# A hybrid attention trunk: 64-row score products of branches A and B become 128-row products

## The chip, the cores and the metric

The kernel runs on one core of a Trainium2 chip. The metric is the device time of one execution in microseconds (us); lower is better. The engines are TensorE (PE in the views, its weight loads PEld), VectorE (DVE), ScalarE (ACT), GpSimd (POOL) and SyncE (SP, whose queue issues the weight transfers).

## The reference

Two layers of an encoder block over 256 tokens of width 2048, in float32. One normalised input feeds three attention branches; each is gated, projected and summed, and an output projection ends the layer. The change touches the scores of branches A and B. Branch A (first lines) has 8 heads of 128 position-free and 64 rotary channels, with one rotary key `kr` for all heads; branch B has 8 heads with two softmax maps (`c`) of 64 channels each:

```python
sc = (jnp.einsum('bqhd,bkhd->bhqk', qn_b, kn)
      + jnp.einsum('bqhr,bkr->bhqk', qr_b, kr)).astype(jnp.float32) * scale
...
sc = jnp.einsum('bqhcd,bkhcd->bhcqk', q_b, k).astype(jnp.float32) * scale
mask = _chunk_causal_mask(i * Q_BLOCK, Q_BLOCK, s_len)
p = jax.nn.softmax(jnp.where(mask, sc, -jnp.inf), axis=-1)
a = p[:, :, 0] - lam * p[:, :, 1]
return jnp.einsum('bhqk,bkhe->bqhe', a.astype(v.dtype), v)
```

Branch C is an attention over 128 channels per head with a position bias. It has no 64-channel part.

## The kernel before, in words

Every product is made from split operands: a value is written as a high part and a low part, each exact in the matmul's input format, and a product of two such values is high times high, high times low and low times high.

The big work is `matunit`: 256 tokens times a weight of K rows and up to 512 columns. Weights come in blocks of 256 rows (512 KB) on SP's queue into four buffers (`wr`). ScalarE rounds a block to its high part (`wh`, L146), VectorE subtracts to get the low part (`wl`, L147), three buffers each, and TensorE makes twelve products of 512 columns from a block (L155 to L157). Each layer runs some fifty such units.

The attention of a branch is done in two halves of four heads. For a half, `qk_natural` and `rope` normalise and rotate queries and keys with tokens in the partitions, `to_transposed` turns them on TensorE (L197), and a split function takes them out of PSUM as high and low parts. Then for each head `scores` (L276) multiplies a stationary query slice of 128 tokens by the keys: 128 key columns for the first 128 tokens, 256 for the second. `softmax_exp` takes the row minimum on VectorE (L287) and the exponential on ScalarE (L289). In branch B, `diff_half` combines the two maps of a head on VectorE (L367); the combined map is transposed (L297) and multiplied by the values (L314).

A head of branch B has only 64 channels per map, so its high and low parts share one 128-row tile. `split_stacked` puts the query's high part in one half of the rows and its low part in the other. `split_twice` puts the key's high part in both halves, so one 128-row product of the two gives (high + low of the query) times the high of the key. The remaining query high times key low is a product of its own, over 64 rows:

```python
q, k = op["q"][m][:, hl, :], op["k"][m][:, hl, :]
return [(q, k), (q[hi], kl[hi, hl, :])]
```

`hi` is the half of the rows that holds the query's high part: rows 0 to 63 for map 0, rows 64 to 127 for map 1. The rotary part of branch A is built in the same way: `krt[:, 0, :]` is the high part of the shared rotary key and `krt[:, 1, :]` its low part. That key is transposed from a tile that already holds it twice, so both parts fill all 128 rows.

In the names, `l0b0` is layer 0, branch B, half 0; `l0b_s` are scores, `l0b0k` the key's high parts, `l0b0kl` its low parts, `l0b0q` the stacked queries, `l0b0z_p` the sums of the gate unit that runs beside the scores, `l0b0z_h` and `l0b0z_l` its split weights.

A scheduler that simulates the timeline fixes the order on each engine when the kernel is built; each engine then runs its own list in order and waits on semaphores. It places scores and transposes between the products of the next `matunit`. Tiles of the attention come from a ring of eleven buffers (`att`), so the twelfth tile waits until the first is read for the last time. Transposes share two PSUM buffers (`ps_t`), scores another two (`ps_s`).

Of the kernel before, what the change touches and what calls it, by code (L numbers as in the profile page):

```python
# [8 lines left out]
F32 = mybir.dt.float32  # L9
F32R = mybir.dt.float32r  # L10
AF = mybir.ActivationFunctionType
# [31 lines left out]
def stream_plan():  # L43
    """The order in which weight blocks are consumed: (source, column selector, K, N)."""
    order = []
    for l in range(DEPTH):
        def win(name, lo, n):
            order.append(("w_in", l, lo, DM, n))
        win("cq", 0, 512)
        win("ckv", 512, 320)  # L50
        win("az", 832, 512)
        order.append(("uq", l, 0, 512, 512))
        order.append(("uq", l, 1024, 512, 512))
        order.append(("ukv", l, 0, 256, 512))
        order.append(("ukv", l, 1024, 256, 512))
        win("az", 832 + 512, 512)
        order.append(("uq", l, 512, 512, 512))
        order.append(("ukv", l, 512, 256, 512))
        order.append(("ukv", l, 1536, 256, 512))
        qb = 1856  # L60
        for hf in range(2):
            for s in (1, 0, 2, 3):
                win("b", qb + s * BW + hf * 512, 512)
        gb = 1856 + 8 * BW
        for j in range(4):
            win("g", gb + j * 512, 512)
            order.append(("br0", l, j * 512, BW, 512))
        qc = 1856 + 4 * BW
        for hf in range(2):
            for s in (1, 0, 2, 3):  # L70
                win("c", qc + s * BW + hf * 512, 512)
        for n in (1, 2):
            for j in range(4):
                win("g", gb + n * DM + j * 512, 512)
                order.append((f"br{n}", l, j * 512, BW, 512))
        for j in range(4):
            order.append(("out", l, j * 512, DM, 512))
    return order
# [3 lines left out]
def trunk_kernel(ctx: ExitStack, tc: tile.TileContext, x, xT, w, cols, rows, tab, bias, ident_d, out):  # L82
    nc = tc.nc
# [19 lines left out]

    # ---------------------------------------------------------------- loads that come first
    colt = const.tile([P, DEPTH, NCOL], F32, name="colt")
# [14 lines left out]

    # keeps the array's clock up while the first loads are on their way
    warm = xgp.tile([P, 512], F32R, tag="xl3", name="warm")
# [4 lines left out]

    # ---------------------------------------------------------------- weight stream
    state = {"off": 0}

    def matunit(lhs, K, N, name, pre=None):
        """x-stationary product [256 tokens, N] over K, three exact passes of split operands."""
        ps = [ps_m.tile([P, 512], F32, tag="mm", name=f"{name}_p{t}") for t in range(NT)]
# [26 lines left out]
    def split(dh, dl, src, gain=None):  # L160
        """dh + dl = src * gain, both representable in float32r."""
        if gain is None:
# [7 lines left out]
    def split_stacked(d0, d1, src, gain=None):  # L170
        """Two 64-row operands of src: d0 = [high; low] of rows 0-63, d1 = [low; high] of rows 64-127."""
        a, b = slice(0, 64), slice(64, P)
# [8 lines left out]

    def split_twice(d0, d1, dl, src, gain):
        """d0 = [high; high] of rows 0-63, d1 the same of rows 64-127, dl the low parts in place."""
        a, b = slice(0, 64), slice(64, P)
        for hi, lo, d in ((a, b, d0), (b, a, d1)):
            nc.scalar.activation(d[hi], src[hi], AF.Copy, scale=gain[hi])
            nc.scalar.activation(d[lo], src[hi], AF.Copy, scale=gain[hi])
            nc.vector.scalar_tensor_tensor(out=dl[hi], in0=src[hi], scalar=gain[hi], in1=d[hi].bitcast(F32),
                                           op0=ALU.mult, op1=ALU.subtract)

    def to_transposed(src, nblk, dh, dl, gain, name, per_block=False, put=None):
        """src(t) [128 tokens, nblk*128] -> dh, dl [128, nblk, 256]; put(blocks, psum) replaces the plain split."""
        for b0 in range(0, nblk, 2):
# [13 lines left out]
    def rstd(ss, n, width, name):  # L207
        """(ss / width + eps) ** -0.5 over [128, n], in place."""
        nc.gpsimd.tensor_scalar(out=ss, in0=ss, scalar1=1.0 / width, scalar2=EPS, op0=ALU.mult, op1=ALU.add)
        nc.gpsimd.tensor_tensor(out=ss, in0=ss, in1=mhalf[:, :n], op=ALU.pow)  # L210

    def qk_natural(ps, gs, rcol, name):
        """per-head RMS normalisation of a [256, 512] product -> two natural tiles."""
        ng = 512 // gs
# [22 lines left out]
    def rope(dst, src, ctab, stab, ng, half, eng, name):  # L237
        """dst = src * ctab + swap(src) * stab over [128, ng, 2*half]."""
        shp = [P, ng, 2 * half]
# [24 lines left out]

    # ---------------------------------------------------------------- attention
    def scores(parts, name):
        """-scores of one head: [128 q, 0:128] for tokens 0-127, [128 q, 128:384] for tokens 128-255.

        parts: (stationary, moving) pairs whose products add up."""
        s = ps_s.tile([P, 384], F32, tag="s", name=name)  # L270
# [11 lines left out]
    def softmax_exp(s, add, mx, sums, name):  # L282
        """exp(score - max) with row sums; add(t) is subtracted from the scores."""
        p = wk.tile([P, 384], F32, tag="p", name=name, bufs=3)
# [8 lines left out]
    def p_transposed(p, name):  # L293
        """p [128 q, 384] -> split [128 k, 384]: columns are (k0, q0), (k0, q1), (k1, q1)."""
        pt = ps_t.tile([P, 512], F32, tag="t", name=f"{name}_pt")
# [7 lines left out]
    def attend(p, vh, vl, hl, name):  # L303
        """p [128 q, 384] times V of head hl of the half -> PSUM [128 q, tile, 128]."""
        ph, pl = p_transposed(p, name)
# [11 lines left out]
    def attend_transposed(p, vh, vl, hl, name):  # L317
        """the same product as PSUM [128 dv, 256 q]."""
        ph, pl = p_transposed(p, name)
# [11 lines left out]
    def simple_half(z, parts, vh, vl, add, name):  # L331
        """softmax attention of four heads -> transposed attention * z [128, 4, 256]."""
        zt = zp.tile([P, HH, SEQ], F32, tag="z", name=f"{name}zt")
# [47 lines left out]

    # ---------------------------------------------------------------- layers
    xg_next = None
# [3 lines left out]
    for l in range(DEPTH):  # L387
# [7 lines left out]

        # the normalised input and its first product
        if l == 0:
# [11 lines left out]
        def first_norm(rcol):  # L409
            """r of the first layer from the transposed x: squares summed over blocks, then over partitions."""  # L410
            acc = wk.tile([P, 384], F32, tag="p", name="xacc", bufs=3)[:, :SEQ]
# [21 lines left out]

        # the layer's gains, rotary tables and lambda
        rowt = wk.tile([P, 2, 512], F32, tag="g", name=f"rowt{l}").rearrange("p a b -> p (a b)")
# [26 lines left out]

        # ------------------------------------------------------------ branch A
        ss = sm.tile([P, NT], F32, tag="sscq", name=f"sscq{l}")
# [61 lines left out]
        for hf in range(2):  # L526
# [21 lines left out]
            def parts(hl):  # L548
                hi = slice((hl % 2) * 64, (hl % 2) * 64 + 64)
                qs = qr[hf][:, (hl % 2) * 2 + hl // 2, :]  # L550
                return three(qh[:, hl, :], ql[:, hl, :], kh[:, hl, :], kl[:, hl, :]) + [
                    (qs, krt[:, 0, :]), (qs[hi], krt[hi, 1, :])]

# [3 lines left out]

        # ------------------------------------------------------------ branch B
        zb = [None, None]
        for hf in range(2):  # L560
            n = f"l{l}b{hf}"
            op = {}
            for i, nm in ((1, "k"), (0, "q")):
# [6 lines left out]
                if nm == "k":  # L570
                    kl = att_tile(f"{n}kl")
                    put = lambda bs, pt: split_twice(d[0][:, bs, :], d[1][:, bs, :], kl[:, bs, :], pt, cg[:, 4:5])
                else:
# [6 lines left out]
            def bparts(hl, m):  # L580
                hi = slice(m * 64, m * 64 + 64)
                q, k = op["q"][m][:, hl, :], op["k"][m][:, hl, :]
                return [(q, k), (q[hi], kl[hi, hl, :])]

            diff_half(zb[hf], bparts, vh, vl, nlam, n)

        # ------------------------------------------------------------ gates, branch products
        yacc = bigp.tile([P, NT, DM], F32, tag="big", name=f"yacc{l}")
# [25 lines left out]

        # ------------------------------------------------------------ branch C
        zc = [None, None]
# [30 lines left out]

        # ------------------------------------------------------------ output projection, residual
        xres = bigp.tile([P, NT, DM], F32, tag="big", name=f"xres{l}")
# [102 lines left out]
```

## Time and profile before

| | |
|---|---|
| median of 3 runs | 2074.09 us (2073.89 to 2075.56) |
| the profiled execution, first to last instruction | 2074.0 us |
| TensorE busy | 2061.1 us, 9612 products |
| TensorE's weight loads busy | 1705.3 us |
| VectorE busy | 1200.8 us |
| ScalarE busy | 1117.7 us |
| GpSimd busy | 230.2 us |

The time that is on record for the profiled execution is its span; it lies 0.1 us from the median, so sums are made against it directly. A product's busy time on TensorE runs past the start of the next one, since products are pipelined; the pace of the engine is read from the distance between starts. A weight load (PEld) belongs to each product and normally runs while the product before it streams.

### The profile page before, as it was taken

How to read it: one execution, taken by the hardware profiler on the slowest of the kernel's cores; microseconds unless marked ns; L12 is line 12 of the kernel's file. 1: busy time of each engine (PE TensorE's matmuls, PEld its weight loads, DVE VectorE, ACT ScalarE, POOL GpSimd, SP SyncE). 2: the span in 40 equal slices, each digit the busy share in tenths (PEclk: the TensorE clock that was granted, in tenths of full speed). 3: DMA queues.
4: the chain of work that ended last, by engine and by line, in shares of the span. 5: the costliest groups of instructions: out<-in, count | busy, mean ns of one | idle time of the engine just before them, and what ended most of it. 6: DMA issues, size and time to landing. Idle time of an engine off the chain costs nothing.

```text
span 2074.0 us, 25839 instructions
## 1 busy us (share of the span) xinstructions
PE 2061.1 (99%) x9612; PEld 1705.3 (82%) x9612; DVE 1200.8 (58%) x1558; ACT 1117.7 (54%) x1606; POOL 230.2 (11%) x373
## 2 busy tenths in 40 slices
PE   8999999999999999999999999999999999999999
PEld 7888787888888888888888887878888888888887
DVE  6666666545655545555557666664455555455554
ACT  6666766444565544445456667564445555444443
POOL 4323032000200000000013130400001000000000
PEclk9999999999999999999999999999999999999999
DMA  6544445455555565556665444545556555655574
GB/s 221 189 153 143 152 156 186 161 193 189 192 170 181 165 197 192 190 191 239 207 190 181 147 148 145 170 163 173 193 187 194 168 181 172 194 193 185 191 243 153
DMA packets 106909, 375.27 MB, mean 181 GB/s; under 512 B 11920, under 2 KB 16016, under 8 KB 106272
## 3 DMA queue, kind: packets, MB, share of 16 engines
q1 hardware_dynamic: 104864, 365.18, 53.7%
q0 software_dynamic: 1920, 8.46, 1.3%
q8 instruction: 75, 1.23, 0.3%
q14 instruction: 50, 0.41, 0.1%
HBM read 369.39 MB, written 4.19 MB: 180 GB/s over the span
## 4 chain that ended last, share of the span: by engine, by line
PE 96%; POOL 1%; ACT 1%; DVE 1%; issue 0%; DMA 0%; SPq 0%; POOLq 0%; ACTq 0%; DVEq 0%
PE l0g_p L155 4%; PE l1g_p L155 4%; PE l1g_p L156 4%; PE l0g_p L156 4%; PE l0g_p L157 4%; PE l1g_p L157 4%; PE l0o_p L155 1%; PE l0o_p L156 1%; PE l0o_p L157 1%; PE l1o_p L155 1%; PE l1o_p L156 1%; PE l1o_p L157 1%; PE l0b_s L276 1%; PE l1b_s L276 1%; PE l0az_p L157 1%; PE l1az_p L156 1%
## 5 line engine op out<-in xcount | busy, mean ns | idle before, releaser
L147 DVE TENSOR_TENSOR l1g_l<-l1g_r,l1g_h 128x1024 fp32r<-128x1024 f32 x96 | 117.4, 1224 | 107.9 <-ACT l1g_h L146 107.8
L147 DVE TENSOR_TENSOR l0g_l<-l0g_r,l0g_h 128x1024 fp32r<-128x1024 f32 x96 | 117.4, 1224 | 107.9 <-ACT l0g_h L146 107.8
L146 ACT CAST l0g_h<-l0g_r 128x1024 fp32r<-128x1024 f32 x96 | 101.1, 1053 | 139.3 <-PE l0g_p L157 86.4
L146 ACT CAST l1g_h<-l1g_r 128x1024 fp32r<-128x1024 f32 x96 | 101.1, 1053 | 139.3 <-PE l1g_p L157 86.4
L156 PE MATMUL l1g_p<-l1g_l,xh 128*128 128x512 f32 x384 | 150.2, 391 | 0.0
L156 PE MATMUL l0g_p<-l0g_l,xh 128*128 128x512 f32 x384 | 150.2, 391 | 0.0
L157 PE MATMUL l1g_p<-l1g_h,xl 128*128 128x512 f32 x384 | 150.0, 391 | 0.0
L157 PE MATMUL l0g_p<-l0g_h,xl 128*128 128x512 f32 x384 | 150.0, 391 | 0.0
L155 PE MATMUL l1g_p<-l1g_h,xh 128*128 128x512 f32 x384 | 136.6, 391 | 0.0
L155 PE MATMUL l0g_p<-l0g_h,xh 128*128 128x512 f32 x384 | 136.6, 391 | 0.0
L155 PEld LDWEIGHTS l1g_p<-l1g_h,xh 128*128 128x128 f32 x384 | 72.0, 188 | 15.0
L155 PEld LDWEIGHTS l0g_p<-l0g_h,xh 128*128 128x128 f32 x384 | 72.1, 188 | 14.9
L157 PEld LDWEIGHTS l0g_p<-l0g_h,xl 128*128 128x128 f32 x384 | 72.1, 188 | 14.7
L157 PEld LDWEIGHTS l1g_p<-l1g_h,xl 128*128 128x128 f32 x384 | 72.1, 188 | 14.8
L156 PEld LDWEIGHTS l0g_p<-l0g_l,xh 128*128 128x128 f32 x384 | 72.1, 188 | 14.6
L156 PEld LDWEIGHTS l1g_p<-l1g_l,xh 128*128 128x128 f32 x384 | 72.1, 188 | 14.6
L147 DVE TENSOR_TENSOR l1o_l<-l1o_r,l1o_h 128x1024 fp32r<-128x1024 f32 x32 | 39.2, 1224 | 41.7 <-ACT l1o_h L146 41.7
L146 ACT CAST l1o_h<-l1o_r 128x1024 fp32r<-128x1024 f32 x32 | 33.8, 1055 | 53.1 <-PE l1o_p L157 45.9
L147 DVE TENSOR_TENSOR l0o_l<-l0o_r,l0o_h 128x1024 fp32r<-128x1024 f32 x32 | 39.2, 1224 | 36.1 <-ACT l0o_h L146 36.1
L146 ACT CAST l0o_h<-l0o_r 128x1024 fp32r<-128x1024 f32 x32 | 33.7, 1054 | 40.8 <-PE l0o_p L157 30.8
L650 POOL DMA_DIRECT2D xres<-x x1 | 0.8, 768 | 316.5 <-PE l0n2j3yT_t L197 316.5
L650 POOL DMA_DIRECT2D xres<-xscr x1 | 0.8, 768 | 316.5 <-PE l1n2j3yT_t L197 316.5
(1632 smaller groups left out, 5985.7 us busy)
## 6 DMA issues: line engine op xcount, KB each, us to landing
l0g_r<-w SPq DMA_DIRECT2D x96, 512.0 KB, 3.4
l1g_r<-w SPq DMA_DIRECT2D x96, 512.0 KB, 3.4
l0o_r<-w SPq DMA_DIRECT2D x32, 512.0 KB, 3.5
l1o_r<-w SPq DMA_DIRECT2D x32, 512.0 KB, 3.8
l0az_r<-w SPq DMA_DIRECT2D x16, 512.0 KB, 3.8
l1az_r<-w SPq DMA_DIRECT2D x16, 512.0 KB, 3.9
l0b0k_r<-w SPq DMA_DIRECT2D x8, 512.0 KB, 3.4
l0b0q_r<-w SPq DMA_DIRECT2D x8, 512.0 KB, 3.4
```

The costliest lines, as they stand in the source:

```text
L146: nc.scalar.copy(wh[:, ks, :N], wr[:, ks, :N])
L147: nc.vector.tensor_tensor(out=wl[:, ks, :N], in0=wr[:, ks, :N], in1=wh[:, ks, :N].bitcast(F32), op=ALU.subtract)
L155: nc.tensor.matmul(ps[t][:, :N], h[:, ts], wh[:, k2, :N], start=first, stop=False)
L156: nc.tensor.matmul(ps[t][:, :N], h[:, ts], wl[:, k2, :N], start=False, stop=False)
L157: nc.tensor.matmul(ps[t][:, :N], lo[:, ts], wh[:, k2, :N], start=False, stop=last)
L276: nc.tensor.matmul(o, a[:, qs], b[:, :kn], start=i == 0, stop=i == len(parts) - 1)
L650: nc.gpsimd.dma_start(xres, x_src.rearrange("(t p) d -> p t d", p=P))
```

## The change

The key's low part, like its high part, is now written to both halves of a 128-row tile, and the last product of each score group takes all 128 rows of the stacked query. The sum gains the product of the two low parts. In branch A the low part is in both halves already, so only the slices go. In branch B `split_twice` writes two tiles of low parts, one for each map, in place of one; its copies and subtractions alternate between ScalarE and VectorE. Comments and docstrings were dropped as well, which the diff leaves out.

```diff
-    def split_twice(d0, d1, dl, src, gain):
+    def split_twice(d0, d1, l0, l1, src, gain):
         a, b = slice(0, 64), slice(64, P)
-        for hi, lo, d in ((a, b, d0), (b, a, d1)):
-            nc.scalar.activation(d[hi], src[hi], AF.Copy, scale=gain[hi])
-            nc.scalar.activation(d[lo], src[hi], AF.Copy, scale=gain[hi])
-            nc.vector.scalar_tensor_tensor(out=dl[hi], in0=src[hi], scalar=gain[hi], in1=d[hi].bitcast(F32),
-                                           op0=ALU.mult, op1=ALU.subtract)
+        for hi, lo, d, dl in ((a, b, d0, l0), (b, a, d1, l1)):
+            for o in (hi, lo):
+                nc.scalar.activation(d[o], src[hi], AF.Copy, scale=gain[hi])
+                nc.vector.scalar_tensor_tensor(out=dl[o], in0=src[hi], scalar=gain[hi],
+                                               in1=d[hi].bitcast(F32), op0=ALU.mult, op1=ALU.subtract)
...
             def parts(hl):
-                hi = slice((hl % 2) * 64, (hl % 2) * 64 + 64)
                 qs = qr[hf][:, (hl % 2) * 2 + hl // 2, :]
                 return three(qh[:, hl, :], ql[:, hl, :], kh[:, hl, :], kl[:, hl, :]) + [
-                    (qs, krt[:, 0, :]), (qs[hi], krt[hi, 1, :])]
+                    (qs, krt[:, 0, :]), (qs, krt[:, 1, :])]
...
                 if nm == "k":
-                    kl = att_tile(f"{n}kl")
-                    put = lambda bs, pt: split_twice(d[0][:, bs, :], d[1][:, bs, :], kl[:, bs, :], pt, cg[:, 4:5])
+                    kl = [att_tile(f"{n}kl{m}") for m in range(2)]
+                    put = lambda bs, pt: split_twice(d[0][:, bs, :], d[1][:, bs, :], kl[0][:, bs, :],
+                                                     kl[1][:, bs, :], pt, cg[:, 4:5])
...
             def bparts(hl, m):
-                hi = slice(m * 64, m * 64 + 64)
-                q, k = op["q"][m][:, hl, :], op["k"][m][:, hl, :]
-                return [(q, k), (q[hi], kl[hi, hl, :])]
+                q = op["q"][m][:, hl, :]
+                return [(q, op["k"][m][:, hl, :]), (q, kl[m][:, hl, :])]
```

VectorE's list where the first half of branch B of layer 0 takes its keys (`l0b0kT_t`) out of PSUM, before the change; L188 writes a key's low part, L147 splits a weight block, L179 writes a query's low part:

```order
L188 SCALAR_TENSOR_TENSOR l0b0kl<-l0b0kT_t_1816,cgain,l0b0k_1813 64x512
L164 TENSOR_TENSOR l0abT1l<-l0a1zt,l0abT1h 128x1024
L147 TENSOR_TENSOR l0b0z_l_2191<-l0b0z_r_2189,l0b0z_h_2190 128x1024
L188 SCALAR_TENSOR_TENSOR l0b0kl<-l0b0kT_t_1816,cgain,l0b0k_1814 64x512
L188 SCALAR_TENSOR_TENSOR l0b0kl<-l0b0kT_t_1827,cgain,l0b0k_1813 64x512
L147 TENSOR_TENSOR l0b0z_l_2209<-l0b0z_r_2207,l0b0z_h_2208 128x1024
L188 SCALAR_TENSOR_TENSOR l0b0kl<-l0b0kT_t_1827,cgain,l0b0k_1814 64x512
L147 TENSOR_TENSOR l0b0z_l_2227<-l0b0z_r_2225,l0b0z_h_2226 128x1024
L179 SCALAR_TENSOR_TENSOR l0b0q_2015<-l0b0qT_t_2017,cgain,l0b0q_2015 64x512
```

The same place after the change:

```order
L188 SCALAR_TENSOR_TENSOR l0b0kl_1815<-l0b0kT_t_1817,cgain,l0b0k_1813 64x512
L147 TENSOR_TENSOR l0b0z_l_2196<-l0b0z_r_2194,l0b0z_h_2195 128x1024
L188 SCALAR_TENSOR_TENSOR l0b0kl_1816<-l0b0kT_t_1817,cgain,l0b0k_1814 64x512
L188 SCALAR_TENSOR_TENSOR l0b0kl_1815<-l0b0kT_t_1830,cgain,l0b0k_1813 64x512
L147 TENSOR_TENSOR l0b0z_l_2214<-l0b0z_r_2212,l0b0z_h_2213 128x1024
L188 SCALAR_TENSOR_TENSOR l0b0kl_1816<-l0b0kT_t_1817,cgain,l0b0k_1814 64x512
L188 SCALAR_TENSOR_TENSOR l0b0kl_1815<-l0b0kT_t_1830,cgain,l0b0k_1813 64x512
L147 TENSOR_TENSOR l0b0z_l_2232<-l0b0z_r_2230,l0b0z_h_2231 128x1024
L188 SCALAR_TENSOR_TENSOR l0b0kl_1816<-l0b0kT_t_1830,cgain,l0b0k_1814 64x512
L147 TENSOR_TENSOR l0b0z_l_2250<-l0b0z_r_2248,l0b0z_h_2249 128x1024
L188 SCALAR_TENSOR_TENSOR l0b0kl_1816<-l0b0kT_t_1830,cgain,l0b0k_1814 64x512
L179 SCALAR_TENSOR_TENSOR l0b0q_2020<-l0b0qT_t_2022,cgain,l0b0q_2020 64x512
```

Eight low-part writes stand there in place of four (the first of the eight just ahead of the piece), and the query's first low part now comes after the fourth weight split, not after the third.

TensorE's list at the first scores of the same half, before the change; `l0b0kl` is the 64-row product:

```order
L155 MATMUL l0b0z_p_2188<-l0b0z_h_2244,xh_1_132 128x512
L276 MATMUL l0b_s_2340<-l0b0k_1813,l0b0q_2015 128x128
L276 MATMUL l0b_s_2340<-l0b0kl,l0b0q_2015 128x128
L156 MATMUL l0b0z_p_2187<-l0b0z_l_2245,xh_1_132 128x512
L157 MATMUL l0b0z_p_2187<-l0b0z_h_2244,xl_1_136 128x512
```

And after the change (the shape in a row is that of the result, so it is 128 by 128 in both):

```order
L155 MATMUL l0b0z_p_2193<-l0b0z_h_2267,xh_2_133 128x512
L276 MATMUL l0b_s_2345<-l0b0k_1813,l0b0q_2020 128x128
L276 MATMUL l0b_s_2345<-l0b0kl_1815,l0b0q_2020 128x128
L156 MATMUL l0b0z_p_2192<-l0b0z_l_2268,xh_2_133 128x512
L157 MATMUL l0b0z_p_2192<-l0b0z_h_2267,xl_2_137 128x512
```

The pair is the same and as many products stand on TensorE as before; it comes one weight block later (the block split as `l0b0z_l_2268` is the fifth of the unit, `l0b0z_l_2245` was the fourth). In branch A TensorE's list is as it was, and SP's list of transfers is the same.

## Rows read from the trace of the kernel before

**Rows 1.** The page's first part: span, then busy time of TensorE.
```profile
span 2074.0 us, 25839 instructions
...
PE 2061.1 (99%) x9612; PEld 1705.3 (82%) x9612; DVE 1200.8 (58%) x1558; ACT 1117.7 (54%) x1606; POOL 230.2 (11%) x373
```

**Rows 2.** Waits of TensorE, whole span: us in total, times, longest.
```profile
PE l0cq_p L156 <- DVE l0cq_l L147: 5.1, 5, 2.2
...
PE l1b1qT_t L197 <- POOL l1b1q_n L250: 0.2, 1, 0.2
```

**Rows 3.** Timeline of TensorE, branch C: start us, us, engine, line, product, shapes.
```profile
556.67 0.28 PE L276 MATMUL l0c_s<-l0c0kl,l0c0qh 128*128 128x128 f32 x1
556.78 0.27 PE L276 MATMUL l0c_s<-l0c0kh,l0c0ql 128*128 128x128 f32 x1
...
557.40 0.28 PE L276 MATMUL l0c_s<-l0c0kh,l0c0qh 128*128 128x256 f32 x1
557.52 0.28 PE L276 MATMUL l0c_s<-l0c0kl,l0c0qh 128*128 128x256 f32 x1
...
558.34 0.39 PE L156 MATMUL l0c0v_p<-l0c0v_l,xh 128*128 128x512 f32 x1
...
559.94 0.39 PE L157 MATMUL l0c0v_p<-l0c0v_h,xl 128*128 128x512 f32 x1
```

**Rows 4.** Timeline of TensorE, first scores of branch B.
```profile
229.87 0.22 PE L276 MATMUL l0b_s<-l0b0k,l0b0q 128*128 128x128 f32 x1
230.02 0.33 PE L276 MATMUL l0b_s<-l0b0kl,l0b0q 64*128 64x128 f32 x1
230.28 0.50 PE L156 MATMUL l0b0z_p<-l0b0z_l,xh 128*128 128x512 f32 x1
230.62 0.40 PE L157 MATMUL l0b0z_p<-l0b0z_h,xl 128*128 128x512 f32 x1
```

**Rows 5.** Timeline of the weight loads there; idle time before in brackets.
```profile
230.02 0.18 PEld L276 LDWEIGHTS l0b_s<-l0b0kl,l0b0q 64*128 64x128 f32 x1 [0.18 <-issue]
230.27 0.19 PEld L156 LDWEIGHTS l0b0z_p<-l0b0z_l,xh 128*128 128x128 f32 x1
```

**Rows 6.** Timeline of TensorE, a 256-column pair of branch B.
```profile
326.56 0.28 PE L276 MATMUL l0b_s<-l0b1k,l0b1q 128*128 128x256 f32 x1
...
327.42 0.40 PE L157 MATMUL l0b1z_p<-l0b1z_h,xl 128*128 128x512 f32 x1
```

**Rows 7.** Timeline of TensorE, first rotary products of branch A.
```profile
117.43 0.53 PE L276 MATMUL l0a_s<-krt,l0a0qr 128*128 128x128 f32 x2
...
118.11 0.28 PE L276 MATMUL l0a_s<-l0a0kl,l0a0qh 128*128 128x256 f32 x1
```

**Rows 8.** Timeline of TensorE, last scores of branch B in layer 1.
```profile
1394.27 0.22 PE L276 MATMUL l1b_s<-l1b1k,l1b1q 128*128 128x128 f32 x1
...
1395.63 0.40 PE L155 MATMUL l1g_p<-l1g_h,xh 128*128 128x512 f32 x1
```

**Rows 9.** Weight loads of line 276: count, ns min/median/max, first and last start, forms.
```profile
L276 PEld LDWEIGHTS l0a_s<-krt,l0a0qr x32: 182/185/192, 117.4 to 185.1; 128*128 128x128 f32 x16, 64*128 64x128 f32 x16
...
L276 PEld LDWEIGHTS l0b_s<-l0b0kl,l0b0q x16: 182/183/183, 230.0 to 266.8; 64*128 64x128 f32 x16
```

**Rows 10.** Line 188 on VectorE: count, ns min/median/max, first and last start.
```profile
L188 DVE SCALAR_TENSOR_TENSOR l0b0kl<-l0b0kT_t,cgain,l0b0k x4: 742/750/759, 213.9 to 221.4; 64x512 fp32r<-64x512 f32 x4
```

**Rows 11.** Windows: busy us of PE, PEld, DVE, ACT, POOL; clock, DMA share, GB/s.
```profile
213.90:226.10 12.20, 12.20 (x61) 10.09 (x60) 9.81 (x11) 11.21 (x15) 0.00 (x0) 1.00 0.53 163
```

**Rows 12.** Timeline of TensorE, branch B: a transpose, the half's last score.
```profile
258.76 0.27 PE L297 MATMUL l0b_pt<-ident,l0b_e 128*128 128x128 f32 x1
...
266.84 0.38 PE L276 MATMUL l0b_s<-l0b0kl,l0b0q 64*128 64x256 f32 x1
```

**Rows 13.** Timeline of VectorE: the combination of two maps, the next half's low part.
```profile
256.81 0.74 DVE L367 SCALAR_TENSOR_TENSOR l0b_e<-l0b_e,l0b_cc,l0b_e 128x128 f32<-128x128 f32 x2
...
297.26 0.74 DVE L188 SCALAR_TENSOR_TENSOR l0b1kl<-l0b1kT_t,cgain,l0b1k 64x512 fp32r<-64x512 f32 x1 [1.49 <-ACT l0b1k L187]
```

## The prediction

> **What bounds the kernel now.** I read the page first. TensorE is busy for 2061.1 of the 2074.0 us of the span, 12.9 us short of it [rows 1]. The waits of TensorE come next: seven groups that add up to 7.9 us, headed by 5.1 us of the very first projection; the last of them is 0.2 us [rows 2]. So TensorE is the bound from start to end, and a change can only save what it takes off TensorE's own queue. Busy time does not say how well that queue runs, since the ends of products are modelled and overlap the next start. What counts is the distance from one start to the next, so the third view is TensorE's timeline.
>
> **The clean pace.** In branch C, whose products all have 128 rows, consecutive score products start 0.11 us apart when 128 columns stream and 0.12 us apart when 256 do; 512-column projection products go 558.34 to 559.94 us for seven of them, 0.229 us each [rows 3]. These three paces are my price list.
>
> **What a 64-row product costs now.** In the first half of branch B a 128-row key product starts at 229.87 us, its 64-row partner at 230.02, the next projection product at 230.28 and the one after it at 230.62 [rows 4]. Three products took 0.75 us; at the clean pace they take 0.11 + 0.11 + 0.23 = 0.45. The excess of 0.30 us is the price of the 64-row product in this place. The view of weight loads shows where it sits: the load of the 64-row product begins only when its matmul does, after 0.18 us in which no load ran, and the next load begins 0.25 us later [rows 5]. Everywhere else the next load runs underneath the product before. So the array empties twice, once ahead of a 64-row product and once behind it.
>
> The same subtraction elsewhere:
> - 256 columns alone, 326.56 to 327.42 us: 0.86 less (0.12 + 0.12 + 0.23) is 0.39 [rows 6].
> - branch A, the two rotary products of 128 columns and the 256-column product behind them, 117.43 to 118.11 us: 0.68 less (0.11 + 0.11 + 0.12) is 0.34 [rows 7].
> - branch B with a 128- and a 256-column pair in a row, 1394.27 to 1395.63 us: 1.36 less (0.22 + 0.24 + 0.23) is 0.67 for two [rows 8].
>
> The row groups of line 276 give the count: a branch A entry carries 16 products with 64 rows, a branch B entry 16 more [rows 9]. There are two entries of A and four of B like these, so 32 + 64 = 96. I made the subtraction over all the 62 places where they stand (rows 7 is the first, rows 8 the last): branch A 11.2 us, branch B 22.6 us, 33.7 us in all, 0.35 us per product.
>
> **The change part by part.**
> - *Products.* All 96 become 128-row products of the same columns in the same count; nothing is added on TensorE. If they run at the clean pace, 33.7 us go. A price of 0.30 for each, the lowest of the four places worked out, would give 29 us; 0.39, the highest, 37. Since every place is in the sum, these are the ends for a single price and not for the total; I take 33.7, and what stays open is the clean pace, at 0.01 us for each of the two or three products of a place some 2 us either way.
> - *Low parts written twice.* Branch B gets four more DVE instructions in each half, 16 in all, of a form that is in the trace at 750 ns [rows 10]: 12 us on DVE. ScalarE keeps its count; only its order against DVE changes. Branch A's key table already holds the low part in both halves, so nothing is added there. The place to look is the first half of B, where in 12.2 us DVE is busy for 9.81 [rows 11]. It has 2.4 us to spare and is given 3.0. The overflow of 0.6 us, once per layer, comes to 1.2 us. It may be hidden: the order puts the query's transposes later, and the weight split stands about one weight block, 12 products or 2.7 us, ahead of TensorE. Bounds are 0 and 12 us, the latter if no DVE instruction is covered; I take 1.0. In the second half DVE has longer pauses while the low parts are made, and I cost the four there at nothing.
> - *Cover that goes.* The drains also gave VectorE and ScalarE time to finish a softmax. The shortest slack of a head in branch B is in the first half: DVE ends the combination at 257.55 us (256.81 + 0.74) and the transpose starts at 258.76, 1.2 us later [rows 12, 13]. With no more than four 64-row products of a later head inside such a chain, the drains cover 1.4 us of it, so a wait of about 0.2 us could appear there. It is the shortest of the eight heads of a layer. I cost it at nothing; the upper bound is half of what branch B wins, 11 us.
> - *Buffers.* The pool of eleven attention tiles now turns by eight, not seven, per half. The second low-part tile of half 1 takes the buffer of half 0's first key tile. Half 0's last score starts at 266.84 us and half 1's first low part is written at 297.26 [rows 12, 13], so 30 us lie between, and this costs nothing.
>
> Sum on the profiled execution: 2074.0 - 33.7 + 1.0 = 2041.3 us. Its span stands 0.1 us from the median of 2074.09, so the forecast for a median is 2041.4.
>
> **A rule against it.** The load of the 64-row product lasts 0.18 us, that of the 128-row product behind it 0.19 [rows 5], so the number of rows makes no difference to a load by itself. The Trainium skill, "TensorE: Matmul & The Clock Gate", section "Why this matters for your kernels", says that one product over 32 rows takes the same time as one over 128. Read by itself that rule gives the change no gain: 2074 us, and it is the second rival below. The Trainium skill's "TensorEngine Tiling (Array Packing)", section "Key Properties", says that going from one row tiling to another drains the engine; by that rule the excess belongs to the alternation, which the change ends. The starts in rows 4 and 5 agree with the second rule, since the excess lies around the 64-row product and not in it.
>
> **The rivals.**
> - *Given back in waits (0.12).* TensorE catches up with VectorE and ScalarE in branch B and stands where it drained before. For it: DVE is at 80% in the stretch of rows 11. Against it: branch C runs with the same kind of order and TensorE has no wait there. If half of branch B's 22.6 us comes back, the time is 2041.4 + 11 = 2052.
> - *Nothing changes (0.03).* The 0.35 us belong to something that both forms share, say the second product into one score group. Against it: the third product of a group in branch C starts 0.11 us after the second [rows 3]. The time would be 2074.
> - *Slower (0.03).* The ring of eleven tiles binds: the low-part write waits on VectorE, in order, for half 0's last score, and every weight split queues behind it. It starts to cost when that score ends 30 us later against the write than now; to lose more than it wins, TensorE would have to stand some 19 us per layer (33.7 + 4.1 over two), which gives 2078 or more.
>
> **How the numbers follow.** The forecast has 0.82, with its own range of 2039 to 2045 (2 us for the clean pace, waits of up to 4 us). The range is 2038 to 2049: the low end lets the saving be 36 us with nothing given back, the high end takes in most of the first rival, short of its full half; it leaves out about 0.13. A change of 0.2%, 4.1 us, is about what a measurement here can tell from none. Faster by more: the forecast and the first rival, 0.94. Within it: the second rival, 0.03. Slower: the third, 0.03.
>
> **What would show it.** Right: no 64-row form is left at line 276, key and low-part products start 0.11 to 0.12 us apart, and the product behind them follows with no gap between loads; 2.7 to 2.9 us come off each A half and 5.6 to 5.7 off each B half. Branch C, the gates and the output projection keep their lengths. Wrong: starts of the new products 0.2 us apart or more, or rows in TensorE's waits that name VectorE or ScalarE in branch B, above all for the weight split behind the key's low parts and for the transposes of the probabilities. If these waits add up to over 8 us, the range fails on the high side.

## The result and the profile after

The changed kernel takes 2042.89 us (median of 4 runs, 2041.53 to 2043.33) against 2074.82 us for the kernel before in the same set (4 runs). The ratio is 0.9845 with a 95% interval of 0.9833 to 0.9857, so 1.4 to 1.7% less. The profiled execution spans 2041.0 us against 2074.0: 33.0 us less, where the prediction had 32.7; by the medians 31.9 us went. The forecast for the median, 2041.4 us in a range of 2038 to 2049, is 1.5 us below what was measured.

The page of the changed kernel, first part (it answers to [rows 1]):

```profile
span 2041.0 us, 25847 instructions
...
PE 2027.4 (99%) x9612; PEld 1694.4 (83%) x9612; DVE 1211.8 (59%) x1574; ACT 1114.8 (55%) x1606; POOL 231.0 (11%) x373
```

TensorE runs the same 9612 products and is still the bound. VectorE gained 16 instructions and 11.0 us of busy time (1211.8 against 1200.8) while the whole became shorter.

TensorE's timeline at the first scores of branch B, and behind it the 256-column pair (they answer to [rows 4] and [rows 6]):

```profile
227.15 0.22 PE L276 MATMUL l0b_s<-l0b0k,l0b0q 128*128 128x128 f32 x1
227.21 0.27 PE L276 MATMUL l0b_s<-l0b0kl,l0b0q 128*128 128x128 f32 x1
227.31 0.45 PE L156 MATMUL l0b0z_p<-l0b0z_l,xh 128*128 128x512 f32 x1
227.60 0.40 PE L157 MATMUL l0b0z_p<-l0b0z_h,xl 128*128 128x512 f32 x1
...
230.10 0.28 PE L276 MATMUL l0b_s<-l0b0k,l0b0q 128*128 128x256 f32 x1
230.22 0.28 PE L276 MATMUL l0b_s<-l0b0kl,l0b0q 128*128 128x256 f32 x1
230.34 0.22 PE L276 MATMUL l0b_s<-l0b0k,l0b0q 128*128 128x128 f32 x1
```

The same three products that took 0.75 us now take 0.45 (227.15 to 227.60), which is the clean price that the prediction worked out from branch C. It is the sum that agrees and not each distance: the pair starts 0.06 us apart, and the projection product behind it takes 0.29 us to the next start in place of 0.23. The 256-column pair goes at 0.12 us a product here.

The weight loads there (they answer to [rows 5]):

```profile
227.15 0.19 PEld L276 LDWEIGHTS l0b_s<-l0b0kl,l0b0q 128*128 128x128 f32 x1
227.26 0.19 PEld L156 LDWEIGHTS l0b0z_p<-l0b0z_l,xh 128*128 128x128 f32 x1
```

The low product's load starts with the product before it, at 227.15, 0.06 us ahead of its own matmul. Before, it started only with its own matmul, after 0.18 us with no load. The next load follows after 0.11 us instead of 0.25.

TensorE's timeline at the first rotary products of branch A (it answers to [rows 7]):

```profile
117.40 0.39 PE L276 MATMUL l0a_s<-krt,l0a0qr 128*128 128x128 f32 x2
...
117.80 0.28 PE L276 MATMUL l0a_s<-l0a0kl,l0a0qh 128*128 128x256 f32 x1
```

0.40 us in place of 0.68. The row groups of line 276 show that no 64-row form is left (they answer to [rows 9]):

```profile
L276 PEld LDWEIGHTS l0a_s<-krt,l0a0qr x32: 187/192/192, 117.3 to 179.9; 128*128 128x128 f32 x32
...
L276 PEld LDWEIGHTS l0b_s<-l0b0kl,l0b0q x16: 187/190/192, 227.1 to 258.3; 128*128 128x128 f32 x16
```

Time came out of branches A and B and nowhere else. Branch C and everything behind it in layer 0 runs from the first product of `l0c0k` to the first of `l1ckv`. Before:

```profile
494.77 0.71 PE L155 MATMUL l0c0k_p<-l0c0k_h,xh 128*128 128x512 f32 x2
1065.97 0.45 PE L155 MATMUL l1ckv_p<-l1ckv_h,xh 128*128 128x320 f32 x2
```

And after:

```profile
478.34 0.71 PE L155 MATMUL l0c0k_p<-l0c0k_h,xh 128*128 128x512 f32 x2
1049.54 0.45 PE L155 MATMUL l1ckv_p<-l1ckv_h,xh 128*128 128x320 f32 x2
```

Both are 571.20 us. The 16.43 us that layer 0 became shorter were gone by 478.34. Layer 1 has the same picture: counted from the first product of `l0ckv`, 32.7 us are gone at the first product of `l1c0k`, and 32.7 at the last product.

TensorE's waits after the change (they answer to [rows 2]):

```profile
PE l0cq_p L156 <- DVE l0cq_l L147: 5.1, 5, 2.2
...
PE l0b_s L276 <- ACT l0b_e L289: 0.3, 1, 0.3
PE l1b_s L276 <- ACT l1b_e L289: 0.3, 1, 0.3
```

Two waits are new, one in each layer: a score in branch B waits for ScalarE's exponential. The waits of the query's transposes for GpSimd, 0.2 us in each layer before, are gone. One more new wait is not in this view; it shows in the starts (see "Cover that goes" below).

### The profile page after: what moved, and what is told of

Read it like the earlier page. It is cut to its first block, busy times and chain, and to the rows that moved or that the text cites. A ratio compares the mean times of both kernels' runs of the same rounds, so it can differ in the third digit from the quotient of the medians.

```text
span 2041.0 us, 25847 instructions
## 1 busy us (share of the span) xinstructions
PE 2027.4 (99%) x9612; PEld 1694.4 (83%) x9612; DVE 1211.8 (59%) x1574; ACT 1114.8 (55%) x1606; POOL 231.0 (11%) x373
## 4 chain that ended last, share of the span: by engine, by line
PE 97%; ACT 2%; DVE 1%; issue 0%; DMA 0%; SPq 0%; ACTq 0%; DVEq 0%
PE l1g_p L155 4%; PE l0g_p L156 4%; PE l1g_p L156 4%; PE l0g_p L157 4%; PE l0g_p L155 4%; PE l1g_p L157 4%; PE l0o_p L156 1%; PE l0o_p L155 1%; PE l0o_p L157 1%; PE l1o_p L156 1%; PE l1o_p L157 1%; PE l1o_p L155 1%; PE l0az_p L157 1%; PE l0az_p L156 1%; PE l0az_p L155 1%; PE l1az_p L156 1%
## 5 line engine op out<-in xcount | busy, mean ns | idle before, releaser
L147 DVE TENSOR_TENSOR l0g_l<-l0g_r,l0g_h 128x1024 fp32r<-128x1024 f32 x96 | 117.4, 1224 | 108.8 <-ACT l0g_h L146 108.8
L147 DVE TENSOR_TENSOR l1g_l<-l1g_r,l1g_h 128x1024 fp32r<-128x1024 f32 x96 | 117.4, 1224 | 108.8 <-ACT l1g_h L146 108.8
L147 DVE TENSOR_TENSOR l1o_l<-l1o_r,l1o_h 128x1024 fp32r<-128x1024 f32 x32 | 39.2, 1225 | 41.6 <-ACT l1o_h L146 41.6
L147 DVE TENSOR_TENSOR l0o_l<-l0o_r,l0o_h 128x1024 fp32r<-128x1024 f32 x32 | 39.2, 1225 | 36.0 <-ACT l0o_h L146 36.0
L146 ACT CAST l0o_h<-l0o_r 128x1024 fp32r<-128x1024 f32 x32 | 33.7, 1054 | 40.8 <-PE l0o_p L157 33.0
```

The lines of the kernel that those rows point to most:

```text
L146: nc.scalar.copy(wh[:, ks, :N], wr[:, ks, :N])
L147: nc.vector.tensor_tensor(out=wl[:, ks, :N], in0=wr[:, ks, :N], in1=wh[:, ks, :N].bitcast(F32), op=ALU.subtract)
```

## The experiments

In the profiled execution of each the granted clock is 0.998 to 0.999 over the span, as before and after. The end of the first weight unit shifts by some 2 us from run to run, and most of it goes with the place of one stretch at half clock (1.2 of 2.4 GHz). Before, the granted clock is 1.00 from 23 to 27 us and 0.58 from 29 to 33, and the second unit starts at 37.76; with B alone it is 0.59 and 1.00, and the second unit starts at 36.24. In both, TensorE had waited 2.17 us for VectorE, up to 23.34 and 23.48 us. In the early place the next such wait takes up most of the loss: TensorE goes on behind it at 28.28 and 28.40 us. The four runs that start it before 37 us have the early place, the other six the late one. Why it falls at the one or the other is not shown. So besides ratio and span each run is given from the first product of the second unit (`l0ckv`) to the last product (`l1o`), both read from TensorE's timeline; the text calls these two starts the marks. The change itself stands in the first two rows:

| kernel | ratio to before (95%) | span | second unit starts | last product starts | between |
|---|---|---|---|---|---|
| before | 1 | 2074.0 | 37.76 | 2068.43 | 2030.67 |
| changed | 0.9845 (0.9833 to 0.9857) | 2041.0 | 37.72 | 2035.67 | 1997.95 |
| A alone | 0.9951 (0.9937 to 0.9965) | 2063.0 | 37.44 | 2057.43 | 2019.99 |
| B alone | 0.9890 (0.9877 to 0.9904) | 2050.3 | 36.24 | 2044.90 | 2008.66 |
| low parts twice, 64 rows kept | 0.9990 (0.9981 to 0.9999) | 2071.5 | 37.52 | 2066.13 | 2028.61 |
| 64-row products side by side | 0.9930 (0.9918 to 0.9943) | 2059.5 | 37.38 | 2054.13 | 2016.75 |
| changed, 32 products of C with 64 rows | 0.9896 (0.9881 to 0.9912) | 2052.6 | 38.06 | 2047.24 | 2009.18 |
| the same with 96 rows | 0.9839 (0.9825 to 0.9852) | 2039.8 | 36.07 | 2034.47 | 1998.40 |
| changed, 64 products of C with 64 rows in 48 places | 0.9925 (0.9912 to 0.9937) | 2057.1 | 36.72 | 2051.77 | 2015.05 |
| as the first of these, 32 rows | one run | 2050.9 | 36.39 | 2045.47 | 2009.08 |

The theory: each stretch of 64-row products between 128-row products costs some 0.35 us, because the array empties on the way in and on the way out; the text calls this a drain. Its rivals: the order that came with the change, the number of rows in a product as such, or a price of each product by itself.

**Branch A alone.** The kernel before with

```diff
-                hi = slice((hl % 2) * 64, (hl % 2) * 64 + 64)
                 qs = qr[hf][:, (hl % 2) * 2 + hl // 2, :]
...
-                    (qs, krt[:, 0, :]), (qs[hi], krt[hi, 1, :])]
+                    (qs, krt[:, 0, :]), (qs, krt[:, 1, :])]
```

> Only branch A's 32 rotary low products take 128 rows; branch B is as before. Drain theory (each 64-row product between 128-row ones costs 0.35 us, and nothing is given back in A): 11.2 us less, a ratio of 0.9946 and a profiled span of about 2062.8. Rival, the gain belongs to the new order that the change brought in branch B: nothing, ratio 1.000, since the lists of all engines are those of before here.

The ratio is 0.9951, and between the two marks 10.7 us are gone (2030.67 less 2019.99). The order is that of before on every engine, so it isn't a new order that brings this.

**Branch B alone.** The changed kernel with branch A's 64-row slices put back.

```diff
+                hi = slice((hl % 2) * 64, (hl % 2) * 64 + 64)
...
-                    (qs, krt[:, 0, :]), (qs, krt[:, 1, :])]
+                    (qs, krt[:, 0, :]), (qs[hi], krt[hi, 1, :])]
```

> Only branch B changes (two low-part tiles, 64 low products of 128 rows); branch A is as before. Drain theory: 22.6 us less, less about 0.9 given back, so 21.7 us, ratio 0.9895, span about 2052.3. If the give-back of the whole change came from branch A, the full 22.6. If branch B loses half of its gain in waits: 11 us, ratio 0.995.

The ratio is 0.9890; between the marks 22.0 us are gone. The two parts add up: 10.7 + 22.0 = 32.7, and the whole change has 32.7 as well (2030.67 less 1997.95). The span alone would mislead here: 1.5 us of its 23.7 us come from an earlier start of the second unit.

**The costs without the gain.** The low parts are written twice and the order is that of the changed kernel, but the products keep 64 rows.

```diff
             def bparts(hl, m):
+                hi = slice(m * 64, m * 64 + 64)
                 q = op["q"][m][:, hl, :]
-                return [(q, op["k"][m][:, hl, :]), (q, kl[m][:, hl, :])]
+                return [(q, op["k"][m][:, hl, :]), (q[hi], kl[m][hi, hl, :])]
```

Branch A's slices are put back as well.

> The key's low part is written twice and the order of all engines is that of the changed kernel, but all 96 low products keep 64 rows: the costs of the change without its gain. Drain theory: between 0 and 1.2 us more than before, ratio 1.000 to 1.0006. If the 16 added writes on VectorE are paid in full: 12 us more, ratio 1.006. If the new order by itself brings time: less than before.

It is not slower but slightly faster, 0.9990 (0.9981 to 0.9999), 2.1 us between the marks. So the 16 added writes and the new order together cost nothing. The run does not tell the two apart, but no wait of TensorE here names the writes. Some 0.7 of the 2.1 us is where the query's transposes no longer wait for GpSimd: before, the transpose at 318.96 us started 0.60 us after the product ahead of it; in this order the distance is 0.23, and it is the same in layer 1. For the rest I have no row.

**64-row products side by side.** The kernel before, with the products of a score group's second tile added in reverse, so that its 64-row product follows that of the first tile:

```diff
-            for i, (a, b) in enumerate(parts):
+            for i, (a, b) in enumerate(parts if t == 0 else parts[::-1]):
```

> The 64-row products stay, but the second tile of each score group adds its products in reverse, so that in 40 of 48 places two 64-row products stand next to one another; 96 places of one become 56 places. Drain theory (the price is paid for going to 64 rows and back): 40 times 0.35, about 14 us less, ratio 0.9932. If each 64-row product has its price by itself, wherever it stands: no change, ratio 1.000.

The ratio is 0.9930; 13.9 us between the marks. TensorE's timeline in branch B, where `x2` is two 64-row products in a row:

```profile
248.38 0.22 PE L276 MATMUL l0b_s<-l0b0k,l0b0q 128*128 128x128 f32 x1
248.53 0.49 PE L276 MATMUL l0b_s<-l0b0kl,l0b0q 64*128 64x128 f32 x2
248.95 0.39 PE L276 MATMUL l0b_s<-l0b0k,l0b0q 128*128 128x256 f32 x1
249.17 0.39 PE L155 MATMUL l0b1k_p<-l0b1k_h,xh 128*128 128x512 f32 x1
```

Four products take 0.79 us, against 0.11 + 0.11 + 0.12 + 0.12 = 0.46 at the clean pace: 0.33 us for two 64-row products together, where two that stand apart cost 0.67 in [rows 8]. The price goes with the place and not with the product.

**64 rows where there were none.** The changed kernel, and in branch C

```diff
-                return three(qh[:, hl, :], ql[:, hl, :], kh[:, hl, :], kl[:, hl, :])
+                return three(qh[:, hl, :], ql[:, hl, :], kh[:, hl, :], kl[:, hl, :])[:2] + [
+                    (ql[0:64, hl, :], kh[0:64, hl, :])]
```

> The changed kernel, and in branch C the last product of each score group (query's low part by key's high part) uses rows 0 to 63 only, so half of that term is left out. 32 products of 64 rows stand alone between products of 128 rows; nothing else differs in instruction or column count. Drain theory: 32 times 0.35 is 11.2 us more than the changed kernel, a span of about 2052, ratio to before 0.990. If the price in A and B came from something else than the rows: 0 more, span 2041, ratio 0.9845.

Between the marks it takes 11.2 us more than the changed kernel (2009.18 less 1997.95). TensorE's timeline:

```profile
547.92 0.22 PE L276 MATMUL l0c_s<-l0c0kl,l0c0qh 128*128 128x128 f32 x1
548.07 0.33 PE L276 MATMUL l0c_s<-l0c0kh,l0c0ql 64*128 64x128 f32 x1
548.33 0.50 PE L156 MATMUL l0c0z_p<-l0c0z_l,xh 128*128 128x512 f32 x1
548.67 0.40 PE L157 MATMUL l0c0z_p<-l0c0z_h,xl 128*128 128x512 f32 x1
```

0.75 us for these three, to the hundredth what [rows 4] show in branch B. Lists and counts are those of the changed kernel, so the rows alone bring it about.

**96 rows.** The same edit with `0:96` in place of `0:64`.

> As e5_c64 but with rows 0 to 95, so a quarter of that term is left out. If what costs is any product with fewer rows than its neighbours: 11.2 us more than the changed kernel, span about 2052. If only the change to 64 rows costs, and 96 rows run as 128: span 2041, ratio to before 0.9845.

The ratio is 0.9839, the same as the changed kernel within the intervals; between the marks it is 0.5 us above it. TensorE's timeline at the same place:

```profile
545.26 0.22 PE L276 MATMUL l0c_s<-l0c0kl,l0c0qh 128*128 128x128 f32 x1
545.32 0.28 PE L276 MATMUL l0c_s<-l0c0kh,l0c0ql 96*128 96x128 f32 x1
545.43 0.45 PE L156 MATMUL l0c0z_p<-l0c0z_l,xh 128*128 128x512 f32 x1
545.71 0.40 PE L157 MATMUL l0c0z_p<-l0c0z_h,xl 128*128 128x512 f32 x1
```

0.45 us, the clean price. A product with fewer rows than its neighbours isn't dear as such; 64 rows are.

**Two of three with 64 rows.**

```diff
-                return three(qh[:, hl, :], ql[:, hl, :], kh[:, hl, :], kl[:, hl, :])
+                return [(qh[:, hl, :], kh[:, hl, :]), (qh[0:64, hl, :], kl[0:64, hl, :]),
+                        (ql[0:64, hl, :], kh[0:64, hl, :])]
```

> As e5_c64, but the second product of a score group in branch C (query's high part by key's low part) has 64 rows as well, so half of two terms is left out. 64 products of 64 rows stand in 48 places, 16 of them with two next to one another. Drain theory, price per place: 48 times 0.35 is 16.8 us more than the changed kernel, span about 2058. If each product has its price by itself: 64 times 0.35 is 22.4 us more, span about 2063.

17.1 us more than the changed kernel between the marks (2015.05 less 1997.95), so 48 places at 0.36, and not 64 products at 0.35, which would be 22.4.

**32 rows.** As the first of the three, with `0:32`.

> As e5_c64 but with rows 0 to 31, so three quarters of that term are left out. If the price is paid for leaving the 128-row form and coming back, whatever the smaller form: 11.2 us more than the changed kernel, as with 64 rows, a span of about 2052. If it grows as rows fall, with the half of the array that stands idle as its measure: 16 to 17 us more.

11.1 us more between the marks. With a quarter of the rows the price is the one of half the rows, 0.35 us for each of 32. It is one run, but its trace gives the same starts: a 128-column product of 32 rows at 546.43 is followed at 546.68 and 547.01, 0.25 and 0.33 us on, as with 64 rows (0.26 and 0.34).

## Why the prediction was right

- *The bound and the price list* held, the list as sums. TensorE set the end before and after, and 0.45 us for three products is what the clean paces of branch C give. Single distances differ from the 0.11 to 0.12 us that were to show it right: over all of branch B, 22 of the 26 pairs of 128 columns that stand together start 0.06 us apart, and of the 28 of 256 columns 16 start 0.17 and 4 start 0.20 us apart. The last is the distance that was named as a sign of being wrong; the sum holds all the same.
- *The size of the gain.* 33.7 us were forecast to go at the drains. From the kernel that has the costs without the gain to the changed one, 30.7 us go between the marks (2028.61 less 1997.95). That is net of 1.5 us of new waits (below), so the drains themselves were worth some 32.2 us. The 1.5 us short lie within the 2 us that the prediction left open for the clean pace. Another 2.1 us had already gone with the new order.
- *The split* of 11.2 us for branch A and 22.6 for branch B came out as 10.7 and 22.0. But the 22.0 hold the 2.1 us of the new order and are net of the waits; at branch B's drains alone some 21.5 us went (2028.61 less 2008.66, and 1.5).
- *The low parts written twice* were given 1.0 us. No run shows that term: with the writes and without the gain the kernel loses nothing. VectorE is indeed fuller where the keys are split, 10.87 us of 12.2 against 9.81 in [rows 11]:

```profile
210.00:222.20 12.20, 12.20 (x59) 10.08 (x59) 10.87 (x12) 9.22 (x12) 0.00 (x0) 1.00 0.56 181
```

  But no row of TensorE's waits in branch B names the writes or a weight split.
- *Cover that goes* was costed at nothing, and this is where the loss is. The kernel with the costs alone and the changed kernel have one and the same order, so their rows can be laid side by side. In layer 0 two places stand out, both in the first half of branch B. At the first a score needs a buffer that ScalarE reads last. With drains, the exponential of the 256 columns ends well before that score; ScalarE, then TensorE:

```profile
253.07 0.47 ACT L289 ACTIVATE l0b_e<-l0b_s,l0b_mx 128x256 f32<-128x256 f32 x1
253.44 0.20 ACT L289 ACTIVATION_READ_ACCUMULATOR l0b_e<-l0b_s,l0b_mx 128x1 f32 x1
...
254.58 0.40 PE L155 MATMUL l0b1k_p<-l0b1k_h,xh 128*128 128x512 f32 x1
254.81 0.22 PE L276 MATMUL l0b_s<-l0b0k,l0b0q 128*128 128x128 f32 x1
```

  Without drains it ends 0.05 us before the score starts:

```profile
246.75 0.47 ACT L289 ACTIVATE l0b_e<-l0b_s,l0b_mx 128x256 f32<-128x256 f32 x1
247.11 0.20 ACT L289 ACTIVATION_READ_ACCUMULATOR l0b_e<-l0b_s,l0b_mx 128x1 f32 x1
...
246.66 0.39 PE L155 MATMUL l0b1k_p<-l0b1k_h,xh 128*128 128x512 f32 x1
247.36 0.33 PE L276 MATMUL l0b_s<-l0b0k,l0b0q 128*128 128x128 f32 x1 [0.31 <-ACT l0b_e L289]
```

  The slack was 1.17 us (254.81 less 253.64). It is used up: the score starts 0.70 us after the product ahead of it in place of 0.23.

  The second place is the chain that the prediction had picked as the shortest, the second head's transposes. With drains, the combination that the first transpose needs ends more than 2 us ahead of it; VectorE, then TensorE:

```profile
258.27 0.35 DVE L367 SCALAR_TENSOR_TENSOR l0b_e<-l0b_e,l0b_cc,l0b_e 128x128 f32<-128x128 f32 x1
...
260.62 0.40 PE L155 MATMUL l0b1k_p<-l0b1k_h,xh 128*128 128x512 f32 x1
260.86 0.27 PE L297 MATMUL l0b_pt<-ident,l0b_e 128*128 128x128 f32 x1
```

  Without drains it ends 0.15 us ahead:

```profile
251.94 0.35 DVE L367 SCALAR_TENSOR_TENSOR l0b_e<-l0b_e,l0b_cc,l0b_e 128x128 f32<-128x128 f32 x1
...
251.91 0.40 PE L155 MATMUL l0b1k_p<-l0b1k_h,xh 128*128 128x512 f32 x1
252.44 0.30 PE L297 MATMUL l0b_pt<-ident,l0b_e 128*128 128x128 f32 x1
```

  The transpose starts 0.53 us after the product ahead of it in place of 0.24. The view of waits does not list this one. From the first product of `l0b0k` to the first of `l0n0j0b` no other two starts of the changed kernel are more than 0.36 us apart, and in the kernel with the costs alone none are; layer 1 shows the same two. Together they take about 0.77 us in a layer, 1.5 us in all. So the prediction named one of the two waits, with the right head and nearly the right size (0.2 us, measured 0.3), and still put nothing for it; the larger one, at the buffers of the scores, it did not look for. Rows of waits that name ScalarE in branch B were a sign of being wrong; they came, with 0.6 us in the view, far from the 8 that would have broken the range.
- *The sum* came out to 0.1 us partly by luck. In place of 33.7 less 1.0, the runs show some 32.2 at the drains, 2.1 from the order, 1.5 lost in waits and nothing for the writes. The main term was right to 5%; the small ones were not, and cancel.
- *Buffers* cost nothing, as said; no wait of TensorE for a tile of the ring appeared, and the low-part writes on VectorE stand behind ScalarE alone, for 0.4 us in a layer.
- *The rule against it* fell. The Trainium skill's "TensorE: Matmul & The Clock Gate", section "Why this matters for your kernels", puts a product over 32 rows at the time of one over 128. The load alone agrees, with 0.18 us for 64 rows against 0.19 for 128 in [rows 5]. The product among 128-row products does not: in the 32-row run each costs 0.35 us more. The Trainium skill's "TensorEngine Tiling (Array Packing)", section "Key Properties", has the drain at a change of the tiling mode, and the section "Available Configurations" there knows 128, 64 and 32 rows, none of 96. The traces agree with both: 64 and 32 rows have the price, 96 have none, and two in a row pay once.
- *The rivals.* Half of branch B given back: shown false, since the new waits take 1.5 us and not 11. No change: shown false by branch A alone and by branch C with 64 rows. The ring that binds: no row of it.

What stays open: why the new order is some 2 us faster with the 64-row products kept, beyond the waits for GpSimd that it ended. And that the array empties is read from the two late loads: the runs show that the price belongs to the place where 128 rows are left and taken up again, but none of them tells an array that empties from a load that merely does not run ahead.

## What to carry to other kernels

Read TensorE from start to start, and price a form against its neighbours: here 96 small products of 9612 hid some 32 of 2074 us behind a busy share of 99%. Where a product over 64 or 32 rows stands between products over 128, fill its rows with something harmless or useful, or else put such products next to one another so that the price is paid once. And when such gaps go, put a price on the chain with the shortest slack, and look for the buffers whose release they covered as well; read both from the distances between starts, since the view of waits can miss one.

## What the runs showed that I had not expected

A product over 96 rows costs what one over 128 costs (0.45 us for the three products at 545.26 us), so the price steps somewhere between 64 and 96 rows and does not grow with the rows left out; 32 rows cost the same 0.35 us as 64. And the end of the first weight unit moved by up to 2.0 us between executions (36.07 to 38.06 us), as much as some of the effects that were tested, with the place of the stretch at half clock.
